# A decoder trunk on one core: the first modulation is loaded at once, summed in fp32, and the transposes of x run two steps ahead

## The chip, the core and the metric

The kernel runs on one core of one Trainium2 chip. The metric is the device time of one execution in microseconds (us); the median of three runs before the change was 2686.47 us, from 2685.94 to 2688.24. The core has a matrix engine (PE, with its weight loads shown apart as PEld), a vector engine (DVE), a scalar engine (ACT), a further engine for general work (POOL, hardly used here) and a queue that issues transfers (SP, shown as SPq). Each engine takes its instructions in the order in which they were written down for it, and waits on semaphores for the others.

## What is computed

Two residual layers. Each has a token mixer (a gated spatial mixer, then dilated attention) and a squared-ReLU MLP, and each of these four sub-layers is modulated by a vector that is computed from c:

```python
def ada_mod(c, w, b):
    m = jax.nn.silu(c) @ w + b
    shift, scale, gate = jnp.split(m, 3, axis=-1)
    return shift[:, None, :], scale[:, None, :], 1.0 + gate[:, None, :]

# first mixer
shift, scale, gate = ada_mod(c, ada_w[i, 0], ada_b[i, 0])
h = x * (1.0 + scale) + shift
uv = jax.nn.gelu(h @ w_in + b_in)
u, v = jnp.split(uv, 2, axis=-1)
v = layer_norm(v, vn_g, vn_b)
...
return (u * z) @ w_out
```

x is 1024 tokens by 1024 features, c has 1024 values, `ada_w[0, 0]` is 1024 by 3072, `w_in` is 1024 by 2048; everything is fp32.

## The kernel before

Everything is tiled by 128: x as eight row tiles `x_0` to `x_7` (128 tokens by 1024), the features as KD = 8 blocks k. Large products are made on PE in three matmuls, with each fp32 operand cut into a high and a low part (`split`, line 104: ACT rounds the high part to the matrix type `fp32r`, DVE subtracts it): high by high, high by low, low by high (`TERMS`). The change is in the first stage of `mixer_a` alone, before and during the products of v (`v_sum`, L475, PSUM tiles `psv`).

What happens there, in order:

- **Modulation columns** (`mods`, L501 on). The first sub-layer's shift and scale are needed as columns (a feature per partition). For each half h of the features, eight tiles of `ada_w` (128 by 2 by 512, 512 KB each: shift and scale side by side) are loaded into a pool of six buffers `adaw`, and DVE adds them up with the weights silu(c): `adaacc += adaw * silu_c[k]` (L509, L511). What is left is a sum over the 128 partitions. `adaacc` is split, and `mod_cols` (L114) lets PE do the sum: eight matmuls for each of shift and scale, with 128 by 128 of `adahi` or `adalo` as the weights and two columns of ones as the moving side (L119, L120, PSUM tiles `psa`), followed by a small addition of the bias on DVE (L124, tiles `ada`).
- **Bias columns.** c and the 64 rows of the biases `ada_b` are loaded into one tile `rows_c`, transposed together on PE (`rows_ct`) and copied to `cols_c`; silu(c) waits for that.
- **Warm-up.** When tile k = 4 of the first half is there, ACT copies a part of it (L513) and PE multiplies it 26 times by ones into a bank that nobody reads (`warm`, L516). These 26 stand in the order written down, ahead of the sums.
- **Transposes and products.** For each block k, PE transposes x (`pst`, L227, four tiles of 128 by 128, or two), ACT applies scale and shift (`h`, L232), ACT rounds (`hT` high, L107), DVE subtracts (`hT` low, L108), and PE multiplies by the weights `winv` of v (L475). `build_hT` does this for one k at a time; the caller alternates it with `v_sum` (`advance`). Two PSUM banks (`tr`) take the transposes and the sums `psa`. Tiles 0 to 3 come first, for k = 0 to 3 (which need the first half of the modulation alone), then tiles 4 and 5 between the loads of the second half, then its sums, then k = 4 to 7 for tiles 0 to 5, then tiles 6 and 7.
- **Row columns.** `rows` (the norms' weights and some biases) is transposed (`rows_t`, L548) and copied to `cols` (L549) near the end of the second half's loads.

The program is written in a framework whose scheduler sets each engine's order from its own estimates; instructions marked `keep_in_program_order` stay in the order in which they were written. After the products of v come the products of u, the spatial mixing, the output projection, the first MLP, attention and the second MLP; the change leaves their code alone.

## Time and profile before

| what | value |
|---|---|
| median of three runs | 2686.47 us |
| the profiled execution's own time | 2688.41 us |
| its span in the profile | 2686.7 us |
| PE busy | 2648.8 us (99%) |
| DVE busy | 1985.0 us (74%) |
| ACT busy | 1383.5 us (51%) |
| first matmul of the products of v | 26.25 us after the span's start |
| first matmul of the products of u | 134.3 us after the span's start |

How to read what follows: a row of a timeline gives the start in us, the length in us, the engine, the line, the operation, the tile written and the tiles read, the shapes, how many follow each other, and in brackets the idle time before it with what ended it. A row of a table of stretches gives the stretch, its length, the busy time of PE, PEld, DVE, ACT and POOL (with the number of instructions), the granted clock of PE (1.00 is full), the share of the transfer engines, and GB/s. PE's matmuls are pipelined, so a row's length is longer than the pace: the pace is read from the starts.

### The profile page before, as it was taken

What the parts mean: (1) busy time and instruction counts of PE and PEld (TensorE: products, weight loads), DVE (VectorE), ACT (ScalarE), POOL (GpSimd) and SP (SyncE); (2) the same over time, 40 slices, a digit from 0 to 9 for tenths busy, and PEclk for the clock granted to TensorE, in tenths of its full rate; (3) what the DMA queues carried; (4) which work ended last, traced back from release to release, by engine and by line L of the source; (5) the groups of instructions that cost most, each with busy time, mean ns of one, the idle gap of its engine ahead of it and who ended that gap; (6) DMA issues with size and microseconds to landing.
All of it is one profiled execution on the core that took longest, in us unless ns stands there. A gap on an engine that the chain in (4) does not pass through costs nothing.

```text
span 2686.7 us, 36966 instructions
## 1 busy us (share of the span) xinstructions
PE 2648.8 (99%) x13204; PEld 2187.0 (81%) x13204; DVE 1985.0 (74%) x3582; ACT 1383.5 (51%) x2626; POOL 103.3 (4%) x189
## 2 busy tenths in 40 slices
PE   7999999999999999999999999999999999999998
PEld 6888878788888888888888888888877788888887
DVE  5896797787888888555556777777658966577877
ACT  3354475555444564433436666666656655553332
POOL 0000000000000001111110000000010000000000
PEclk9999999999999999999999999999999999999999
DMA  7643346777967645655565544554783654495562
GB/s 275 188 149 94 118 146 226 225 234 256 356 209 253 219 165 188 220 188 180 178 216 157 148 137 130 139 147 136 230 220 111 207 201 157 145 313 192 180 208 83
DMA packets 335069, 505.29 MB, mean 188 GB/s; under 512 B 51692, under 2 KB 168852, under 8 KB 334884
## 3 DMA queue, kind: packets, MB, share of 16 engines
q1 hardware_dynamic: 318500, 444.20, 52.1%
q0 software_dynamic: 16384, 58.73, 6.1%
q8 instruction: 103, 1.69, 0.3%
q14 instruction: 82, 0.67, 0.1%
HBM read 365.92 MB, written 136.92 MB: 187 GB/s over the span
## 4 chain that ended last, share of the span: by engine, by line
PE 86%; DVE 8%; DMA 3%; ACT 2%; issue 1%; SPq 0%; DVEq 0%; ACTq 0%
PE psd L1007 22%; PE psv L1336 13%; PE psua L845 9%; PE psk L1437 7%; PE psq L1437 6%; PE psuc L845 4%; PE psu L636 3%; PE psv L475 3%; PE pv L1606 3%; PE psd_wout L391 3%; PE sc L1526 3%; DMA adaw<-in_ada_w_dram 2%; PE psub L845 2%; PE pT L1579 1%; DVE left L108 1%
## 5 line engine op out<-in xcount | busy, mean ns | idle before, releaser
L845 PE MATMUL psua<-right,left 128*128 128x512 f32 x1536 | 365.5, 391 | 2.3 <-DVE right L108 1.7
L1007 PE MATMUL psd<-rhi,lhi 128*128 128x512 f32 x896 | 349.7, 390 | 0.0
L1007 PE MATMUL psd<-rlo,lhi 128*128 128x512 f32 x896 | 348.8, 389 | 0.0
L1007 PE MATMUL psd<-rhi,llo 128*128 128x512 f32 x896 | 348.6, 389 | 0.0
L845 PEld LDWEIGHTS psua<-right,left 128*128 128x128 f32 x1536 | 286.2, 188 | 67.2 <-DVE right L108 4.2
L1548 ACT ACTIVATE p<-p,stat 128x128 f32<-128x128 f32 (+1 forms) x384 | 168.7, 441 | 97.0 <-DVE stat L1546 97.0
L1007 PEld LDWEIGHTS psd<-rhi,lhi 128*128 128x128 f32 x896 | 168.2, 188 | 35.8 <-ACT part L876 0.9
L1007 PEld LDWEIGHTS psd<-rhi,llo 128*128 128x128 f32 x896 | 168.2, 188 | 35.2
L1007 PEld LDWEIGHTS psd<-rlo,lhi 128*128 128x128 f32 x896 | 168.2, 188 | 34.5
L845 PE MATMUL psuc<-right,left 128*128 128x512 f32 x768 | 188.1, 392 | 0.3 <-ACT part L850 0.2
L845 PEld LDWEIGHTS psuc<-right,left 128*128 128x128 f32 x768 | 142.7, 188 | 33.0 <-DVE right L108 1.8
L108 DVE TENSOR_TENSOR pTlo<-pT,pThi 128x512 fp32r<-128x512 f32 (+1 forms) x160 | 99.3, 621 | 76.5 <-ACT pThi L107 75.5
L107 ACT CAST left<-ws 128x512 fp32r<-128x512 f32 x128 | 79.4, 621 | 139.4 <-DVE ws L765 101.8
L108 DVE TENSOR_TENSOR llo<-lraw,lhi 128x1024 fp32r<-128x1024 f32 x112 | 136.4, 1219 | 2.3 <-ACT lhi L107 2.3
L108 DVE TENSOR_TENSOR left<-ws,left 128x512 fp32r<-128x512 f32 x128 | 88.1, 690 | 65.7 <-ACT left L107 63.5
L144 DVE SCALAR_TENSOR_TENSOR adaacc<-adaw,silu_c,adaacc 128x512 f32<-128x512 f32 x140 | 104.6, 747 | 42.2 <-DMA adaw<-in_ada_w_dram 41.4
L1437 PE MATMUL psk<-form_L,wqk_hi 128*128 128x512 f32 x384 | 126.9, 412 | 0.0
L1437 PE MATMUL psq<-form_L,wqk_hi 128*128 128x512 f32 x384 | 126.4, 410 | 0.0
L1336 PE MATMUL psv<-vrhi,form_S 128*128 128x512 f32 x384 | 119.9, 390 | 1.1 <-DVE vpart L1302 0.6
L107 ACT CAST lhi<-lraw 128x1024 fp32r<-128x1024 f32 x112 | 117.2, 1048 | 7.2 <-PE psd L1007 3.3
L1546 DVE CUSTOM_DVE_ANT_0 p<-sc,bias 128x128 f32<-128x128 f32 (+1 forms) x384 | 113.6, 346 | 7.0 <-PE sc L1526 6.8
L107 ACT CAST pThi<-pT 128x512 fp32r<-128x512 f32 (+1 forms) x160 | 84.8, 530 | 62.3 <-PE pT L1579 45.3
(333 smaller groups left out, 6075.8 us busy)
## 6 DMA issues: line engine op xcount, KB each, us to landing
lraw<-forms SPq DMA_DIRECT2D x112, 512.0 KB
adaw<-in_ada_w_dram SPq DMA_DIRECT2D x160, 256.0 KB
up<-in_mlp_w_up_dram SPq DMA_DIRECT2D x64, 512.0 KB
forms<-s SPq DMA_DIRECT2D x128, 256.0 KB
rraw<-in_mlp_w_down_dram SPq DMA_DIRECT2D x64, 512.0 KB
forms<-part SPq DMA_DIRECT2D x96, 256.0 KB
v<-vs POOLq DMA_DIRECT2D x48, 512.0 KB, 3.6
vraw<-in_b_w_qkv_dram SPq DMA_DIRECT2D x42, 512.0 KB
```

Source lines behind the costliest of these rows:

```text
L107: first = A.copy(hi, src) if hi_engine is A else hi_engine.tensor_copy(hi, src)
L108: return first, lo_engine.tensor_tensor(lo, src, hi, op=ALU.subtract)
L144: ins = V.scalar_tensor_tensor(acc[:], raw[:], silu_c[:, k : k + 1], acc[:], ALU.mult, ALU.add)
L391: T.matmul(p[:], stat[a][:, k, o : o + P], u[b][:, w], start=n == 0, stop=n == count - 1)
L475: T.matmul(sums[i][:], hT[half][a_][:, k, o : o + P], units[c, k // 2][b_][:, n : n + HALF], start=k + a_ + b_ == 0, stop=k == KD - 1 and ...
L636: T.matmul(p[:], wu[a_][:, k * P : (k + 1) * P], hT[half][b_][:, k, :], start=k + a_ + b_ == 0, stop=k == KD - 1 and a_ == 1)
L845: T.matmul(acc, w[:, a, k, :], right[p][:, b, k, :], start=p in (1, 2, 5) and k + a + b == 0, stop=k == 3 and a == 1, skip_group_check=True)
L1007: ins = T.matmul(sums[kind, m][:], l[a][:, k, m * P : (m + 1) * P], r[b][:, k, :], start=p in (1, 5, 2, 3) and kp + k + a + b == 0, stop=k ...
L1336: T.matmul(acc, rows[:, m * P : (m + 1) * P], cols_, start=p in (1, 2, 5) and kp + k + a + b == 0, stop=kp == 1 and k == 1 and a == 1, ski ...
L1437: T.matmul(p[:], wu[a][:, k * P : (k + 1) * P], h_op(k, half, b), start=k + c_ == 0, stop=k == KD - 1 and c_ == 2)
L1546: V.tensor_tensor_reduce(out=pr, in0=banks[e][:, sl], in1=st["bias"][:, width - w :], scale=-0.125, scalar=3e38, op0=ALU.add, op1=ALU.min, ...
L1548: A.activation(pr, pr, AF.Exp, bias=nm, scale=-1.0, accum_out=l)
```

## The change

The diff does five things.

- The eight `ada_w` tiles of the first half go into `vz` (the tile that later holds v and is still unused), so that none of the loads waits for a buffer. Those of the second half have the six buffers `adaw` to themselves.
- c and the biases come in two transfers and two transposes: `rows_c` holds c alone, the biases go into `rows_b`, are loaded behind tile 5, transposed as `rows_bt` and copied to a tile `cols_b` of their own.
- The sums over the partitions are plain fp32 matmuls on `adaacc` itself, with one column of ones (`one`): four for each of shift and scale instead of eight, and no split. Both go into one PSUM bank instead of two.
- The warm-up waits for tile 3 instead of tile 4.
- `in_turn` replaces `advance`: the transposes, h and hT of step m + 2 are written behind the products of step m, tiles 4 and 5 following on tiles 0 to 3 in one sequence. The first transpose of each step is kept in program order.

The core of the diff:

```diff
-        nc.sync.dma_start(rows_c[KD : KD + 64, :], ada_b.rearrange("i s (q p) -> (i s) q p", p=P)[:, 0 : 2 * KD, :])
+            if lo is None:
+                T.matmul(pst[:, 2 * k : 2 * k + 1], hi[:, w], one[:], start=True, stop=True)
+                continue
             T.matmul(pst[:, 2 * k : 2 * k + 2], hi[:, w], ones_r[:, 0:2], start=True, stop=False)
             T.matmul(pst[:, 2 * k : 2 * k + 2], lo[:, w], ones_r[:, 0:2], start=False, stop=True)
...
+            def in_turn(*runs):
+                todo = [(i0, n, k) for i0, n, ks in runs for k in ks]
+                gens = {(i0, n): rows_of(i0, n)(ks) for i0, n, ks in runs}
+                def rows(m):
+                    if m < len(todo):
+                        next(gens[todo[m][:2]])
+                rows(0)
+                rows(1)
+                for m, (i0, n, k) in enumerate(todo):
+                    for i in range(i0, i0 + n):
+                        v_sum(0, i, k)
+                    rows(m + 2)
+                    yield
...
-                        raw = ada0.tile([P, 2, HALF], F32, name=f"adaw_0_{h}_{k}", tag="adaw", bufs=6)
+                        raw = ada0.tile([P, 2, HALF], F32, name=f"adaw_0_{h}_{k}", tag="adaw", bufs=6) if h else \
+                            vz[:, k, :].rearrange("p (t n) -> p t n", t=2)
...
-                        if h == 0 and k == 4:
+                        if h == 0 and k == 3:
                             A.copy(warm, raw[:, 0, :])
...
-                    for part in (1, 0):
-                        split(hi[:, part, :], lo[:, part, :], acc[:, part, :])
-                    for part in (1, 0):
-                        mod_cols(0, part, h, bank("tr", f"psa_{part}_{h}"), hi[:, part, :], lo[:, part, :])
+                    p = bank("tr", f"psa_{h}")
+                    for part in (1, 0):
+                        mod_cols(0, part, h, p[:, 8 * part : 8 * part + 8], acc[:, part, :])
...
+                def bias_cols():
+                    nc.sync.dma_start(rows_b[0:64, :], ada_b.rearrange("i s (q p) -> (i s) q p", p=P)[:, 0 : 2 * KD, :])
+                    pt = bank("tr", "rows_bt")
+                    T.transpose(pt[:, 0:P], rows_b[:], ident[:])
+                    V.tensor_copy(cols_b[:], pt[:, 0:64])
-                mods(0)
+                mods(0, {5: [bias_cols]})
```

Beyond the products of v's first half and the first products of its second half, PE, DVE, ACT and SP have the same instructions in the same order as before. Inside that part the order moves. Three places matter.

**DVE, first half of the modulation.** The names: `adaacc` is the running sum, `vz` in the new rows is a tile of `ada_w`. Before:

```order
L80 COPY cols_c<-rows_ct 128x72
L83 TENSOR_TENSOR silu_c<-cols_c,sg 128x8
L509 TENSOR_SCALAR adaacc_144<-adaw_0_0_145,silu_c 128x1024
L511 SCALAR_TENSOR_TENSOR adaacc_144<-adaw_0_1_148,silu_c,adaacc_144 128x1024
L511 SCALAR_TENSOR_TENSOR adaacc_144<-adaw_0_2_151,silu_c,adaacc_144 128x1024
L511 SCALAR_TENSOR_TENSOR adaacc_144<-adaw_0_3_154,silu_c,adaacc_144 128x1024
L511 SCALAR_TENSOR_TENSOR adaacc_144<-adaw_0_4_157,silu_c,adaacc_144 128x1024
L511 SCALAR_TENSOR_TENSOR adaacc_144<-adaw_0_5_188,silu_c,adaacc_144 128x1024
L511 SCALAR_TENSOR_TENSOR adaacc_144<-adaw_0_6_191,silu_c,adaacc_144 128x1024
L511 SCALAR_TENSOR_TENSOR adaacc_144<-adaw_0_7_194,silu_c,adaacc_144 128x1024
L108 TENSOR_TENSOR adalo_198<-adaacc_144,adahi_197 128x512 x2
```

and after, on the same engine:

```order
L81 COPY cols_c<-rows_ct 128x8
L84 TENSOR_TENSOR silu_c<-cols_c,sg 128x8
L533 TENSOR_SCALAR adaacc_150<-vz,silu_c 128x1024
L535 SCALAR_TENSOR_TENSOR adaacc_150<-vz,silu_c,adaacc_150 128x1024 x5
L557 COPY cols_b<-rows_bt 128x64
L535 SCALAR_TENSOR_TENSOR adaacc_150<-vz,silu_c,adaacc_150 128x1024 x2
L128 SCALAR_TENSOR_TENSOR ada_1_0_204<-psa_199,cols_b 128x4
```

A copy out of PSUM (`cols_b<-rows_bt`) now stands between tile 5 and tile 6 of the sum, and the subtraction of the split is gone.

**PE at the same place.** Before (`psa_0_203` and `psa_0_214` are scale and shift; the rows go on with the low parts in turn):

```order
L79 MATMUL rows_ct<-ident,rows_c 128x128
L516 MATMUL warm<-hT_1_0_131,ones_r 128x512 x26
L119 MATMUL psa_0_203<-ones_r,adahi_197 128x2
L119 MATMUL psa_0_214<-ones_r,adahi_197 128x2
L120 MATMUL psa_0_203<-ones_r,adalo_198 128x2
```

and after:

```order
L80 MATMUL rows_ct<-ident,rows_c 128x128
L540 MATMUL warm<-hT_1_0_133,ones_r 128x512 x26
L556 MATMUL rows_bt<-ident,rows_b 128x128
L121 MATMUL psa_199<-one,adaacc_150 128x1 x8
L231 MATMUL pst_0_0_230<-ident,x_0_139 128x128
```

The transpose of the biases stands behind the 26 warm-up matmuls and ahead of the sums; the last four of the eight sums wait for DVE a second time, for the `ada` of the first four, since both share a bank.

**DVE and PE around the second half of the modulation.** Before, on DVE:

```order
L511 SCALAR_TENSOR_TENSOR adaacc_337<-adaw_1_6_425,silu_c,adaacc_337 128x1024
L108 TENSOR_TENSOR hT_1_1_132<-h_4_2_381,hT_1_0_131 128x256
L108 TENSOR_TENSOR hT_1_1_132<-h_4_3_403,hT_1_0_131 128x256
L511 SCALAR_TENSOR_TENSOR adaacc_337<-adaw_1_7_428,silu_c,adaacc_337 128x1024
L549 COPY cols<-rows_t 128x128
L108 TENSOR_TENSOR adalo_432<-adaacc_337,adahi_431 128x512 x2
```

After, on DVE:

```order
L109 TENSOR_TENSOR winv_3_lo<-winv_3_raw,winv_3_hi 128x1024
L109 TENSOR_TENSOR hT_1_1_134<-h_4_3_373,hT_1_0_133 128x256
L575 COPY cols<-rows_t 128x128
L535 SCALAR_TENSOR_TENSOR adaacc_298<-adaw_1_6_404,silu_c,adaacc_298 128x1024
L535 SCALAR_TENSOR_TENSOR adaacc_298<-adaw_1_7_407,silu_c,adaacc_298 128x1024
L128 SCALAR_TENSOR_TENSOR ada_1_1_415<-psa_410,cols_b 128x4
```

and after, on PE:

```order
L574 MATMUL rows_t<-ident,rows 128x128
L479 MATMUL psv_4_346<-winv_1_hi,hT_1_0_133 128x512
L479 MATMUL psv_4_346<-winv_1_lo,hT_1_0_133 128x512
L479 MATMUL psv_5_350<-winv_1_hi,hT_1_0_133 128x512
L479 MATMUL psv_4_346<-winv_1_hi,hT_1_1_134 128x512
L479 MATMUL psv_5_350<-winv_1_lo,hT_1_0_133 128x512
L479 MATMUL psv_5_350<-winv_1_hi,hT_1_1_134 128x512
L121 MATMUL psa_410<-one,adaacc_298 128x1 x4
L231 MATMUL pst_0_4_436<-ident,x_0_139 128x128
L231 MATMUL pst_0_4_436<-ident,x_1_140 128x128
L231 MATMUL pst_0_4_436<-ident,x_2_141 128x128
L121 MATMUL psa_410<-one,adaacc_298 128x1 x4
```

The copy `cols<-rows_t` stood behind the last tile of the sum and now stands ahead of its last two; the transpose that it waits for stands six products ahead of the sums `psa`.

48 lines of the change are left out of this document (22 added, 26 removed).

## The prediction

> **What bounds the kernel now.** I read the page's first part, then the stretches of the first 100 us, then the timelines of the engines there.
>
> ```profile
> PE 2648.8 (99%) x13204; PEld 2187.0 (81%) x13204; DVE 1985.0 (74%) x3582; ACT 1383.5 (51%) x2626; POOL 103.3 (4%) x189
> 0.00:20.00 20.00, 7.15 (x22) 5.58 (x23) 11.49 (x16) 3.25 (x5) 0.70 (x6) 1.00 0.88 310
> 20.00:40.00 20.00, 19.37 (x96) 15.66 (x95) 14.12 (x18) 10.01 (x16) 0.00 (x0) 0.91 1.01 359
> 40.00:60.00 20.00, 19.32 (x85) 15.71 (x84) 9.00 (x15) 9.77 (x16) 0.00 (x0) 0.83 0.74 235
> 60.00:80.00 20.00, 18.34 (x87) 14.04 (x86) 13.56 (x23) 11.26 (x24) 0.00 (x0) 1.00 0.36 112
> 80.00:100.00 20.00, 20.00 (x98) 16.34 (x98) 19.35 (x31) 10.15 (x18) 3.26 (x4) 1.00 0.54 163
> ```
>
> PE is the bound: of 2686.7 us it is idle for 37.9, and 12.85 + 0.63 + 0.68 + 1.66 = 15.8 of these lie in the first 80 us. From 80 us on it is full, and from a little later its order is unchanged, so what the first stage gains or loses on PE should reach the end whole. The granted clock is below 1 in two of the stretches; that is the other loss here. PE's timeline shows the places:
>
> ```profile
> 13.30 8.04 PE L516 MATMUL warm<-hT,ones_r 128*128 128x512 f32 x26 [7.62 <-ACT hT L513]
> 21.18 0.28 PE L119 MATMUL psa<-ones_r,adahi 128*128 128x2 f32 x2
> 26.25 0.78 PE L475 MATMUL psv<-winv_hi,hT 128*128 128x512 f32 x1
> 45.57 0.27 PE L548 MATMUL rows_t<-ident,rows 128*128 128x128 f32 x1
> 46.95 0.25 PE L119 MATMUL psa<-ones_r,adahi 128*128 128x2 f32 x1
> 47.40 0.25 PE L119 MATMUL psa<-ones_r,adahi 128*128 128x2 f32 x1
> 48.26 0.35 PE L120 MATMUL psa<-ones_r,adalo 128*128 128x2 f32 x1
> 48.48 0.35 PE L119 MATMUL psa<-ones_r,adahi 128*128 128x2 f32 x1
> 48.90 4.01 PE L227 MATMUL pst<-ident,x 128*128 128x128 f32 x16
> 52.57 0.78 PE L475 MATMUL psv<-winv_hi,hT 128*128 128x512 f32 x1
> 57.52 0.61 PE L475 MATMUL psv<-winv_hi,hT 128*128 128x512 f32 x2
> 63.64 0.61 PE L475 MATMUL psv<-winv_hi,hT 128*128 128x512 f32 x2
> 72.00 0.60 PE L227 MATMUL pst<-ident,x 128*128 128x128 f32 x4
> ```
>
> The reader should see two stretches without products, 21.18 to 26.25 and 45.57 to 52.57, in which sums, transposes, h and hT follow one another with nothing beside them. Four stretches show the clock's edges:
>
> ```profile
> 23.80:24.00 0.20, 0.20 (x3) 0.20 (x4) 0.20 (x1) 0.20 (x1) 0.00 (x0) 0.95 0.82 317
> 27.20:27.40 0.20, 0.20 (x2) 0.15 (x1) 0.20 (x2) 0.20 (x1) 0.00 (x0) 0.52 0.98 358
> 47.80:48.00 0.20, 0.20 (x3) 0.20 (x3) 0.16 (x1) 0.00 (x0) 0.00 (x0) 0.69 0.00 0
> 54.60:54.80 0.20, 0.20 (x3) 0.16 (x2) 0.00 (x0) 0.20 (x1) 0.00 (x0) 0.75 0.98 338
> ```
>
> The rows are stretches of 0.2 us; 0.95 means that the clock was at half for a tenth of it. So it falls to half at 23.98, 2.8 us after the warm-up, and at 47.86, 2.3 us after the last product, and comes back at 27.39 and 54.70, 1.1 and 2.1 us after products resume. The sums do not hold it up.
>
> **Loads at once.** The transfers were already full:
>
> ```profile
> 1.76 0.80 SPq L74 DMA_DIRECT2D rows_c<-in_ada_b_dram  x1
> 7.21 2.04 SPq L507 DMA_DIRECT2D adaw<-in_ada_w_dram  x2
> 4.00:5.00 1.00, 0.00 (x0) 0.00 (x0) 0.00 (x0) 0.00 (x0) 0.00 (x0) 1.00 0.67 159
> 8.00:9.00 1.00, 0.00 (x0) 0.00 (x0) 0.86 (x1) 0.00 (x0) 0.00 (x0) 1.00 1.02 324
> 12.63 0.62 ACT L513 CAST hT<-adaw 128x512 fp32r<-128x512 f32 x1 [6.43 <-DMA adaw<-in_ada_w_dram]
> 10.07 5.27 DVE L511 SCALAR_TENSOR_TENSOR adaacc<-adaw,silu_c,adaacc 128x1024 f32<-128x1024 f32 x4 [1.22 <-DMA adaw<-in_ada_w_dram]
> 15.93 2.60 DVE L511 SCALAR_TENSOR_TENSOR adaacc<-adaw,silu_c,adaacc 128x1024 f32<-128x1024 f32 x2 [0.59 <-DMA adaw<-in_ada_w_dram]
> ```
>
> SP's wait for a buffer at 7.21 starves nothing: the engines' share is 1.02 right after it. What is gained is the issue of the biases, 0.80 us, which now stands behind tile 5 and left the hole of 0.67 at 4 to 5 us. The warm-up waits for tile 3 instead of 4: tiles 2 and 4 landed at 10.07 and 12.63, so one tile is worth 1.28. Together the warm-up starts 2.1 earlier, at 11.2, and if it takes as long as before, PE is free at 21.18 - 2.1 = 19.1. Cost of the other transfers: nothing, as they keep their order behind the same bytes; the SP queue waits for `winv` buffers as before.
>
> **The first new wait.** PE could do the sums at 19.1, but DVE cannot have finished adding. The copy of the biases stands between tiles 5 and 6, and waits for a transpose that is queued behind all 26 warm-up matmuls. The same kind of pair, `rows_t` and its copy, is the price:
>
> ```profile
> 45.88 0.29 DVE L549 COPY cols<-rows_t 128x128 f32<-128x128 f32 x1 [0.79 <-PE rows_t L548]
> 22.28 0.16 DVE L124 SCALAR_TENSOR_TENSOR ada<-psa,cols_c 128x4 f32<-128x4 f32 x1 [1.76 <-PE psa L120]
> ```
>
> 19.1 + 0.31 (45.57 to 45.88) + 0.29 = 19.7, then tiles 6 and 7, 2.60: DVE ends at 22.3 instead of 18.53, and the first sum starts at 22.4 instead of 21.18. The removed split costs nothing now and saves nothing: it lay under the warm-up.
>
> **The sums in fp32.** Before, 32 matmuls at a pace of 0.113 us at full clock (four from 46.95 to 47.40) and 0.215 at half (48.26 to 48.48). No row shows a plain fp32 matmul that isn't a transpose. One pass, as for these rows, is the lower end; the upper end is both operands in two parts, four products, 0.45 and 0.86. I take three products, 0.34 and 0.645, because the nearest thing the trace has to a product of two uncut fp32 operands is the kernel's own, three matmuls for each (L475). The clock is at half by then: the warm-up ends at 19.1, and 2.8 later is 21.9. So 8 x 0.645 = 5.2. Between shift and scale PE waits for DVE's `ada`, a matmul's length 0.25 + 0.16 + two hand-overs of 0.05, about 0.5. The sums end at 28.1. The first four transposes stand behind them (0.25 each at half clock, by the row of 16, + 0.25 until the result is there): 29.3. Then ACT:
>
> ```profile
> 21.59 1.05 ACT L107 CAST winv_hi<-winv_raw 128x1024 fp32r<-128x1024 f32 x1 [0.18 <-DMA winv_raw<-in_a_w_in_dram]
> 50.11 1.64 ACT L232 ACTIVATE h<-pst,ada,ada 128x512 f32<-128x512 f32 x2 [3.85 <-PE pst L227]
> 51.65 1.12 ACT L107 CAST hT<-h 128x512 fp32r<-128x512 f32 x2
> ```
>
> h 0.82, the second `winv` cast, which ACT's new order has between h and hT, 1.05, and hT 0.56: the first product starts at 31.8 instead of 26.25, **+5.5**. With one pass it is 28.3 (+2.1), with four products 33.5 (+7.3).
>
> On the price, the Trainium skill ("FP8 and Floating Point Precision", TensorE Precision Notes) says that true fp32 takes four passes through the array. By it the upper end holds, and the sum is that of the first rival below; no run shown here bears it out or contradicts it.
>
> **Products, tiles 0 to 5, k = 0 to 3.** Before 45.57 - 26.25 = 19.32. After: 72 matmuls at 0.227 (27 from 57.52 to 63.64), 16.3; 16 transposes at 0.11 (the four at 72.00: 0.60 less one's length of 0.27, by three), since eight of the sixteen that stood ahead of the first product now stand between products, 1.8; half of about 1.6 us at half clock, 0.8; `rows_t` 0.1. That is 19.0, **-0.3**. The stalls before each group vanish, but the transposes that come in take their place:
>
> ```profile
> 38.81 0.89 PE L227 MATMUL pst<-ident,x 128*128 128x128 f32 x4 [0.44 <-ACT h L232]
> 65.65 0.89 PE L227 MATMUL pst<-ident,x 128*128 128x128 f32 x4 [0.50 <-ACT h L232]
> 73.38 0.44 PE L227 MATMUL pst<-ident,x 128*128 128x128 f32 x2 [0.77 <-ACT h L232]
> ```
>
> **The second new wait.** DVE's last two tiles of the second half now stand behind `cols<-rows_t`, and `rows_t` on PE stands six products, 1.36 us, before the products' end E. DVE: E - 1.36 + 0.31 + 0.29 + 2.60 = E + 1.85; before, the last of these tiles had ended just ahead of `rows_t`:
>
> ```profile
> 43.81 1.28 DVE L511 SCALAR_TENSOR_TENSOR adaacc<-adaw,silu_c,adaacc 128x1024 f32<-128x1024 f32 x1
> 46.09 1.28 DVE L108 TENSOR_TENSOR adalo<-adaacc,adahi 128x512 fp32r<-128x512 f32 x2
> ```
>
> So the split's wait (until 47.37) is replaced by one of the same size. Four sums, at full clock until E + 2.5 and at half after it, end at E + 3.95; three transposes fill the hand-over, 0.75; four more sums, 2.6, E + 7.3; `ada` 0.45; h, h, hT 0.82 + 0.82 + 0.56 and 0.1: E + 10.05. Before 52.57 - 45.57 = 7.0: **+3.05** (one pass -0.5, four products +4.75).
>
> **The rest of the stage**, 52.57 to 72.00 = 19.43: 16.3 + 16 transposes 1.8 + half clock 0.8 + 0.5 for DVE, which now has gelu's neighbours ahead of hT: 19.4, **0**. Tiles 6 and 7 begin as before with their first two steps bare (the 0.77 stays). After that PE is full either way.
>
> **Sum**: 5.5 - 0.3 + 3.05 + 0 = +8.3. The profiled execution took 2688.41 (span 2686.7 + 1.7 around), 1.9 above the median; the sum is a difference, so it goes on the median: 2686.5 + 8.3 = **2694.8**.
>
> **Rivals.**
> 1. Four products for an fp32 matmul: 7.3 - 0.3 + 4.75 = +11.75, 2698.2. For it: an uncut operand on both sides; against it: one column of ones needs no second part.
> 2. One pass at half clock: 2.1 - 0.3 - 0.5 = +1.3, 2687.8. Or three products, but with the clock falling late: the first sums 2.7 at full clock, so the first product at 29.3 (+3.1), and in the second place E + 7.85 (+0.85): +3.65, 2690.1. For it: the low clock lasted 3.41 us (23.98 to 27.39) and 6.84 us (47.86 to 54.70), once and twice the same, as if it were judged in steps of 3.4 us; then 2.3 and 2.8 after the last dense work are two draws, and a fall up to 6.8 after it, the end of the first whole step without work, is possible. Against it: both draws were early, and it cannot stay up, since PE is without products for over 7 us. The Trainium skill ("TensorE: Matmul & The Clock Gate", What's actually happening) says that the clock is judged in windows of about 3.4 us that run free of the program; the two widths agree.
> 3. The change doesn't slow the kernel: a sum is one pass, and so short that the clock falls only behind the first sums. First product at 27.0 (+0.75), -0.3, and E + 6.05 in the second place (-0.95): -0.5, 2686.0. It decides when an fp32 sum costs under 0.2 us. For it: `psa`'s rows show that the pace doesn't depend on two columns; against it: those are rows of the matrix type, for which the kernel cuts its operands.
> 4. The first part doing nothing (transfers hidden anyway) is in the sum already.
>
> **Chances.** 0.2% of 2686.5 is 5.4 us, about what a measurement of this kernel can tell from no change: slower means above 2691.9. My forecast 0.42, of which 0.04 stays below 2691.9; rival 1 0.24; rival 2 0.16; rival 3 0.07; gains that I don't see, such as the idles at 72 to 74 us closing and DVE's first wait being shorter, 0.08; losses above 2700 0.03. Faster: 0.08. Same: 0.16 + 0.07 + 0.04 = 0.27. Slower: 0.38 + 0.24 + 0.03 = 0.65. The range reaches from just under rival 3, 2685.5, to 2700, rival 1 with 2 us for a clock that comes back later; it leaves out about 0.13. The likeliest case alone spans 2691 to 2698.
>
> **What would show it.** The copy to `cols_b` waiting several us for PE and the last two tiles of the sum behind it, the first sum after 22 us; the starts of `psa` giving the price; the granted clock at 0.50 through them; first `psv` near 32; `psa` of the second half starting about 2 us after the products end; no idle before the transposes in between. I am wrong if an fp32 sum is a one-pass matmul, if the clock falls late, or if PE's later idle time swallows the delay.

## The result: slower by 0.5%

| | before | after |
|---|---|---|
| median of four runs, us | 2687.02 (2685.94 to 2688.24) | 2699.35 (2698.19 to 2702.61) |
| ratio after/before, 95% interval | | 1.0052, 1.0041 to 1.0064 |
| profiled execution, us | 2688.41 (span 2686.7) | 2698.19 (span 2696.5) |
| half clock in the first 100 us of the profile, us | 10.24 | 17.07 |
| first product of v | 26.25 | 30.17 |
| 72nd product (the last of tiles 0 to 5 before the second sums) | 45.34 | 50.63 |
| first product after the second sums | 52.57 | 58.06 |
| 144th product (the last of tiles 0 to 5) | 71.77 | 78.42 |
| 288th product | 110.73 | 119.31 |
| 384th product (the end of v) | 133.91 | 142.46 |

The medians differ by 12.3 us, the two profiled executions by 9.8. The forecast was +8.3 with a range up to 2700.0: the side was right, the size was too small, and the ratio applied to 2686.47 gives 2700.4, just above the range. "n-th product" is the start of the n-th matmul of `psv` in a profile; between the 72nd and the next, the second sums stand.

The first part of the page of after, and its stretches:

```profile
PE 2653.1 (98%) x13205; PEld 2189.0 (81%) x13205; DVE 1981.7 (73%) x3581; ACT 1382.1 (51%) x2622; POOL 104.0 (4%) x189
...
0.00:20.00 20.00, 8.79 (x26) 6.77 (x27) 8.22 (x14) 2.11 (x3) 0.70 (x6) 1.00 0.90 314
20.00:40.00 20.00, 15.45 (x66) 12.73 (x65) 10.18 (x13) 7.08 (x10) 0.00 (x0) 0.74 0.79 268
40.00:60.00 20.00, 16.72 (x81) 12.93 (x81) 12.70 (x18) 8.46 (x15) 0.00 (x0) 0.87 0.62 209
60.00:80.00 20.00, 19.22 (x89) 15.10 (x87) 9.67 (x17) 10.94 (x20) 0.00 (x0) 0.95 0.51 176
80.00:100.00 20.00, 19.16 (x94) 14.74 (x94) 15.92 (x27) 12.91 (x23) 1.16 (x2) 1.00 0.55 169
100.00:120.00 20.00, 19.06 (x86) 15.44 (x85) 17.18 (x26) 3.76 (x7) 1.79 (x3) 1.00 0.56 168
```

Between 20 and 40 us PE was busy for 15.45 us where it had 19.37, and at 0.74 of the full clock where it had 0.91. Between 80 and 120 us, where PE was full before, it is idle for 0.84 + 0.94 = 1.78 us. PE's busy time also grew, by 4.3 us, with one matmul more: the same work, more of it at half clock.

PE's timeline of after, the rows that answer to those of before:

```profile
11.66 8.95 PE L540 MATMUL warm<-hT,ones_r 128*128 128x512 f32 x26 [6.79 <-ACT hT L537]
20.44 0.27 PE L556 MATMUL rows_bt<-ident,rows_b 128*128 128x128 f32 x1
23.54 1.23 PE L121 MATMUL psa<-one,adaacc 128*128 128x1 f32 x8 [2.83 <-DVE adaacc L535]
25.03 1.86 PE L121 MATMUL psa<-one,adaacc 128*128 128x1 f32 x8 [0.26 <-DVE ada L128]
26.75 1.95 PE L231 MATMUL pst<-ident,x 128*128 128x128 f32 x8
30.17 0.79 PE L479 MATMUL psv<-winv_hi,hT 128*128 128x512 f32 x1 [1.47 <-ACT hT L108]
...
52.87 1.02 PE L121 MATMUL psa<-one,adaacc 128*128 128x1 f32 x8 [1.84 <-DVE adaacc L535]
...
58.06 0.79 PE L479 MATMUL psv<-winv_hi,hT 128*128 128x512 f32 x1 [1.43 <-ACT hT L108]
...
78.65 0.60 PE L231 MATMUL pst<-ident,x 128*128 128x128 f32 x4
80.84 0.50 PE L479 MATMUL psv<-winv_hi,hT 128*128 128x512 f32 x1 [1.59 <-ACT hT L108]
...
105.55 0.50 PE L170 MATMUL psa<-adahi,ones_r 128*128 128x512 f32 x1 [0.94 <-ACT adahi L108]
```

The reader should see the two waits for DVE ahead of `psa` (2.83 and 1.84 us), and that eight sums take 8 + 8 rows: an fp32 sum is two matmuls, at a pace of 0.11 us each at full clock and 0.215 at half.

DVE's timeline of after shows what the two waits are:

```profile
20.75 0.22 DVE L557 COPY cols_b<-rows_bt 128x64 f32<-128x64 f32 x1 [5.01 <-PE rows_bt L556]
20.89 2.60 DVE L535 SCALAR_TENSOR_TENSOR adaacc<-vz,silu_c,adaacc 128x1024 f32<-128x1024 f32 x2
...
49.59 0.42 DVE L109 TENSOR_TENSOR hT<-h,hT 128x256 fp32r<-128x256 f32 x1
49.92 0.28 DVE L575 COPY cols<-rows_t 128x128 f32<-128x128 f32 x1
50.12 2.60 DVE L535 SCALAR_TENSOR_TENSOR adaacc<-adaw,silu_c,adaacc 128x1024 f32<-128x1024 f32 x2
```

The first copy waits 5.01 us for PE. The second waits for nothing; more on that at the second experiment. The clock's edges in after, by stretches of 0.2 us (it falls in the first and third row and comes back in the second and fourth):

```profile
24.20:24.40 0.20, 0.20 (x3) 0.20 (x3) 0.00 (x0) 0.00 (x0) 0.00 (x0) 0.67 0.88 184
34.40:34.60 0.20, 0.20 (x2) 0.14 (x2) 0.00 (x0) 0.00 (x0) 0.00 (x0) 0.73 1.11 379
54.90:55.10 0.20, 0.20 (x3) 0.20 (x3) 0.00 (x0) 0.00 (x0) 0.00 (x0) 0.72 0.00 0
61.70:61.90 0.20, 0.20 (x2) 0.20 (x1) 0.00 (x0) 0.00 (x0) 0.00 (x0) 0.71 1.11 430
```

It is half from 24.27 to 34.51 and from 54.99 to 61.81. After the first product it stays half for 4.3 us (1.1 before), after the first of the second part for 3.7 us (2.1 before).

### The profile page after: what moved, and what is told of

It is laid out like the page before. It is cut to its first block, busy times and chain, and to the rows that moved or that the text cites. A ratio compares the mean times of both kernels' runs of the same rounds, so it can differ in the third digit from the quotient of the medians.

```text
span 2696.5 us, 36953 instructions
## 1 busy us (share of the span) xinstructions
PE 2653.1 (98%) x13205; PEld 2189.0 (81%) x13205; DVE 1981.7 (73%) x3581; ACT 1382.1 (51%) x2622; POOL 104.0 (4%) x189
## 4 chain that ended last, share of the span: by engine, by line
PE 68%; issue 17%; DVE 7%; DMA 4%; ACT 2%; POOL 2%; SPq 0%; POOLq 0%; DVEq 0%; ACTq 0%
PE psd L1028 19%; PE psua L866 10%; PE psk L1458 7%; PE psq L1458 6%; PE psuc L866 5%; PE pv L1627 3%; PE psd_wout L395 3%; PE sc L1547 3%; PE psv L479 3%; PE psub L866 2%; PE psu L657 2%; DMA adaw<-in_ada_w_dram 2%; PE pT L1600 1%; POOL v L1334 1%; PE psoa L1831 1%
## 5 line engine op out<-in xcount | busy, mean ns | idle before, releaser
L109 DVE TENSOR_TENSOR llo<-lraw,lhi 128x1024 fp32r<-128x1024 f32 x112 | 136.1, 1217 | 2.3 <-ACT lhi L108 2.3
```

The source lines that it names most:

```text
L109: return first, lo_engine.tensor_tensor(lo, src, hi, op=ALU.subtract)
```

## The experiments

Four groups of theories are tested. A: what costs are PE's waits, which DVE's order sets. B: the fp32 sums cost. C: the order of products and transposes costs ("the turns" below: `in_turn`). D: what costs is the half clock. All kernels were timed against runs of the kernel before on the same chip (medians there 2682.8 to 2685.4 us). "Half" is the time at half clock in the first 100 us of the kernel's profile, "384th" the start of the last product of v there (132.5 and 132.4 in two further profiles of the kernel before or its like, 133.9 in the first).

| kernel | ratio to before, 95% | us against before | 384th, us | half, us |
|---|---|---|---|---|
| before, profiled first | | | 133.91 | 10.24 |
| before_again | 1.0000, 0.9992 to 1.0009 | 0.0 | 132.55 | 6.83 |
| after | 1.0052, 1.0041 to 1.0064 | 14.0 | 142.46 | 17.07 |
| again (after once more) | 1.0053, 1.0040 to 1.0067 | 14.2 | 143.74 | 20.48 |
| bias_late | 1.0037, 1.0024 to 1.0051 | 9.9 | 138.74 | 13.65 |
| both_late | 1.0033, 1.0020 to 1.0046 | 8.9 | 138.65 | 13.65 |
| fill | 1.0043, 1.0030 to 1.0056 | 11.5 | 137.87 | 10.24 |
| split | 1.0051, 1.0039 to 1.0064 | 13.7 | 141.66 | 17.07 |
| t67 | 1.0037, 1.0024 to 1.0050 | 9.9 | 139.58 | 17.07 |
| late_t67 | 1.0027, 1.0016 to 1.0037 | 7.2 | 135.23 | 13.65 |
| late_t67_fill | 1.0026, 1.0015 to 1.0036 | 7.0 | 135.33 | 10.24 |
| loads | 1.0017, 1.0009 to 1.0026 | 4.6 | 137.61 | 13.65 |
| sums | 1.0017, 1.0008 to 1.0026 | 4.6 | 133.59 | 6.83 |
| turns | 1.0020, 1.0011 to 1.0029 | 5.4 | 137.32 | 13.65 |
| loads_sums_late | 1.0009, 0.9999 to 1.0018 | 2.4 | 133.24 | 6.83 |
| lsl_64 | 1.0007, 0.9997 to 1.0017 | 1.9 | 132.78 | 3.41 |
| lsl_64_fill | 1.0001, 0.9992 to 1.0010 | 0.3 | 131.24 | 0.00 |
| delay | 1.0000, 0.9991 to 1.0009 | 0.0 | 132.91 | 0.00 |
| before_32 | 1.0005, 0.9996 to 1.0014 | 1.3 | 132.43 | 6.83 |
| after_64 | 1.0046, 1.0033 to 1.0058 | 12.3 | 142.65 | 17.07 |

The third column is the ratio less one, times the median of the kernel before on that chip; an interval of 0.0009 to each side is 2.4 us. "Half" counts from the first record of the clock, which lies between 13.76 and 18.26 us, when the clock comes up during the warm-up. The warm-up does not start at the same time in every execution (10.50 to 13.45 us over the 20 profiles), so a part of a difference between two profiles can lie there.

### The wait for the biases (bias_late)

DVE's copy of the biases is written behind the eighth tile and kept there; DVE, PE and ACT are otherwise as in after.

```diff
                     rows_bt.append(bank("tr", "rows_bt"))
                     T.transpose(rows_bt[0][:, 0:P], rows_b[:], ident[:])
-                    V.tensor_copy(cols_b[:], pt[:, 0:64])
-                mods(0, {5: [bias_cols]})
+                mods(0, {5: [bias_cols], 7: [lambda: tc.keep_in_program_order(V.tensor_copy(cols_b[:], rows_bt[0][:, 0:64]))]})
```

> The changed kernel, with DVE's copy of the biases moved behind the eighth tile of the first sum; nothing else moves. Theory A (the waits cost): the eighth tile is added by 19 us, the first sum starts right behind the transpose of the biases at 20.8 instead of 23.5, the first product comes 3 to 4.5 us earlier (near 26), and the whole is 3.5 to 5 us less than the changed kernel: 8 to 9.5 us above the kernel before. Theory D (what costs is the half clock, whose windows run free): the first product comes earlier as in A, but the clock falls all the same, more of the products are done at half clock, and of the 3.5 to 5 us half or less arrives: 10 to 13 us above the kernel before.

DVE's timeline and PE's, of this kernel:

```profile
9.25 9.21 DVE L535 SCALAR_TENSOR_TENSOR adaacc<-vz,silu_c,adaacc 128x1024 f32<-128x1024 f32 x7
20.86 0.23 DVE L562 COPY cols_b<-rows_bt 128x64 f32<-128x64 f32 x1 [2.40 <-PE rows_bt L560]
```

```profile
20.55 0.27 PE L560 MATMUL rows_bt<-ident,rows_b 128*128 128x128 f32 x1
20.66 0.95 PE L121 MATMUL psa<-one,adaacc 128*128 128x1 f32 x8
21.86 1.05 PE L121 MATMUL psa<-one,adaacc 128*128 128x1 f32 x8 [0.26 <-DVE ada L128]
```

The eighth tile is added at 18.46, the first sum starts at 20.66, the first product at 25.73 instead of 30.17, and both groups of sums run at full clock. Of these 4.4 us 3.7 are left at the 384th product (138.74 against 142.46), and 4.1 in the ratio (14.0 less 9.9). The gain is the 3.5 to 5 us of A, though the 9.9 lies between A's 8 to 9.5 and D's 10 to 13, and the interval of the ratio covers both. The wait was real, and it is the larger of the two waits; one stretch of 3.41 us at half clock went with it (13.65 us instead of 17.07).

### The wait for `cols` (both_late)

The copy `cols<-rows_t` too is put behind the eighth tile, of the second sum.

```diff
-                then[4].append(row_cols)
+                then[7] = [row_cols]
```

> As the last, and the copy of the transposed rows of ln and biases also behind the eighth tile of the second sum. Theory A: the 1.8 to 2.7 us in which PE waits for DVE at 51 us vanish too, the second sums start within 0.3 us of the end of the first products, 6 us above the kernel before (5 to 7.5). Theory D: 9 to 11 us above it, as the shorter gap does not save a window of half clock.

It gained nothing: 0.09 us at the 384th product. PE still waited 1.64 us, as DVE's and PE's timelines of this kernel show:

```profile
45.79 0.42 DVE L109 TENSOR_TENSOR hT<-h,hT 128x256 fp32r<-128x256 f32 x1
46.12 2.60 DVE L535 SCALAR_TENSOR_TENSOR adaacc<-adaw,silu_c,adaacc 128x1024 f32<-128x1024 f32 x2
48.64 0.28 DVE L578 COPY cols<-rows_t 128x128 f32<-128x128 f32 x1
```

```profile
48.87 1.02 PE L121 MATMUL psa<-one,adaacc 128*128 128x1 f32 x8 [1.64 <-DVE adaacc L535]
```

So the copy was not the cause of more than 0.2 us of it, and theory A was wrong here on the mechanism; the 8.9 in the total is near D's 9 to 11. In DVE's order the last two tiles stand behind `winv_lo` and the subtraction for the last `hT` of tiles 4 and 5; with or without the copy they start about 1 us before the products end, and take 2.60. DVE's queue is at fault, but with other instructions in it. Where the tiles stand ahead, in the kernel sums (below), they are done before the products end:

```profile
44.87 2.59 DVE L516 SCALAR_TENSOR_TENSOR adaacc<-adaw,silu_c,adaacc 128x1024 f32<-128x1024 f32 x2
47.38 0.42 DVE L110 TENSOR_TENSOR hT<-h,hT 128x256 fp32r<-128x256 f32 x1
```

There the gap from the last product to the next is 53.24 - 48.68 = 4.6 us; here it is 53.67 - 47.23 = 6.4, in after 58.06 - 51.02 = 7.0. That the place of the tiles makes this difference is read from the comparison; no run moves the tiles alone.

### Work in PE's waits (fill)

The waits of after stay; 12, 6 and 10 matmuls that nobody reads are put into them.

```diff
+                    for _ in range(12 if h == 0 else 10):
+                        tc.keep_in_program_order(T.matmul(pw[:] if h == 0 else p[:, P:HALF], ones_r[:], warm if h == 0 else warm[:, P:HALF], start=True, stop=True))
...
                 rows(0)
                 rows(1)
+                if fill:
+                    for _ in range(6):
+                        tc.keep_in_program_order(T.matmul(fill[0][:], ones_r[:], warm, start=True, stop=True))
```

> The changed kernel with its waits as they are, but matmuls of the warm-up's kind put into them: 12 behind the transpose of the biases, 6 behind the first eight transposes of x, 10 narrower ones ahead of the second sums; their results are not used. Theory D: the clock stays up or is half in one window of 3.4 us instead of five, the first sums and transposes take half the time (first product 1 to 2 us earlier), the products' first 4 us and the 3.7 us after 58 run at full clock: 5 to 6 us less than the changed kernel, 6.5 to 8 us above the kernel before. Theory A: PE's waits are as long, so nothing is gained: 12 to 14 us above the kernel before.

Half clock fell from 17.07 to 10.24 us, the first product came at 27.39, and the 384th 4.6 us earlier than in after. But 2.24 us of that were there before any of the added matmuls could matter. This execution had begun its warm-up 1.05 us earlier, at 10.61, and its clock came up as early as 13.76, so that DVE had the biases and the sum sooner and the first sum started at 21.30 instead of 23.54:

```profile
18.22 3.06 PE L548 MATMUL warm<-hT,ones_r 128*128 128x512 f32 x12
21.30 1.05 PE L121 MATMUL psa<-one,adaacc 128*128 128x1 f32 x8
27.39 0.41 PE L479 MATMUL psv<-winv_hi,hT 128*128 128x512 f32 x1
```

```profile
18.65 2.60 DVE L538 SCALAR_TENSOR_TENSOR adaacc<-vz,silu_c,adaacc 128x1024 f32<-128x1024 f32 x2
```

From the first sum to the 384th product fill gains 2.35 us on after, without any wait taken away, and as much is seen in the total (14.0 less 11.5 = 2.5, with intervals that overlap). That is about half of D's 5 to 6; the 11.5 lies between D's 6.5 to 8 and A's 12 to 14. The fillers ahead of the second sums did not keep the clock up (half from 51.31 to 58.13). Late in the run a wait for a transfer was 4.5 us long here (2.24 in after), with 6.83 us of half clock behind it. D holds for a part of the first stage; in the whole it is not resolved.

### The order for tiles 6 and 7 (t67)

Only this loop gets the old order back, not pinned.

```diff
-            for _ in in_turn((6, 2, range(KD))):
+            gen = rows_of(6, 2, pinned=False)(range(KD))
+            for k in range(KD):
+                next(gen)
+                for i in (6, 7):
+                    v_sum(0, i, k)
                 tick()
```

> The changed kernel with the old order for tiles 6 and 7 alone, where the scheduler may again put products of v's second half between them. Theory A: from the 144th to the 288th product it takes 39.0 us, as in the kernels before, loads and sums, where all kernels with turns took 40.9; the total falls by 2 us: 10 to 11 us above the kernel before. If the order there is not the cause: 40.9 again and 12 to 13 us above it.

From the 144th to the 288th product it took 116.43 - 77.50 = 38.93 us. In the kernel before this is 110.73 - 71.77 = 38.96, in after 119.31 - 78.42 = 40.89. That is the 39.0 expected, and the total falls to 9.9 (10 to 11 expected). PE is full again; stretches of t67:

```profile
80.00:100.00 20.00, 20.00 (x99) 16.05 (x100) 18.29 (x31) 12.81 (x23) 1.72 (x3) 1.00 0.60 185
100.00:120.00 20.00, 20.00 (x90) 16.52 (x89) 16.49 (x26) 3.69 (x6) 1.47 (x2) 1.00 0.54 171
```

Where the scheduler is free it puts products of v's second half between those of tiles 6 and 7, and PE has something to do while ACT makes `hT` and `adahi`. With the steps pinned in turn it waits 1.78 us in these 40 us. All 20 profiles show the 2 us: each kernel that has the turns for tiles 6 and 7 took 40.8 to 41.0 us there, each without them 38.8 to 39.0.

### Each part alone (loads, sums, turns)

Three kernels put one part of the change on the kernel before: loads (the first modulation in `vz`, the biases apart, the warm-up at tile 3), sums (fp32, no split), turns (`in_turn` in all its places).

```diff
+                            vz[:, k, :].rearrange("p (t n) -> p t n", t=2)
...
-                        if h == 0 and k == 4:
+                        if h == 0 and k == 3:
...
-                mods(0)
+                mods(0, {5: [bias_cols]})
```

```diff
-                    for part in (1, 0):
-                        split(hi[:, part, :], lo[:, part, :], acc[:, part, :])
+                    p = bank("tr", f"psa_{h}")
+                        mod_cols(0, part, h, p[:, 8 * part : 8 * part + 8], acc[:, part, :])
```

```diff
-                gen = rows_of(0, 4)(first_ks)
-                for k in first_ks:
-                    advance(gen, k, range(4))
+                turns = in_turn((0, 4, first_ks), (4, 2, first_ks))
...
+            for _ in in_turn((6, 2, range(KD))):
```

> Only the loads part on the kernel before: first modulation into the region of v, biases loaded and copied apart between tiles 5 and 6, warm-up after tile 3; split sums and the old order stay. Theory A (the loss comes from the copy of the biases, which makes DVE wait for a transpose behind the warm-up, and from the low clock that follows): the last two tiles end near 23.5 us as in the changed kernel, the split then stands bare behind them, the first sum starts at 24.2 or later instead of 21.2, all sums are at half clock, the first product comes 4 to 6 us later than before: 2691.5 us (2690 to 2694). Theory B (the loss comes from the uncut fp32 sums): this kernel has none, it starts earlier: 2684 to 2687. Theory C (the loss comes from the products in turn): the same as B.

> Only the fp32 sums on the kernel before, without splits. Theory A: the first sum still starts at 21.2 behind the warm-up, eight sums take 1.8 at full clock or 3.5 at half where sixteen matmuls and two results took 3.9; the second place loses the split of 1.3 us and starts its sums right behind the products: 2 to 3 us less in all, 2684 us (2682.5 to 2687, the clock's windows making up the width). Theory B: 2692 us or more. Theory C: 2686.5.

> Only the transposes two steps ahead of the products on the kernel before, in the order that pins them. Theory A: the first products start with eight transposes instead of sixteen ahead of them, 0.5 to 1 us earlier, and the stage of tiles 0 to 5 is otherwise as long; the stage of tiles 6 and 7 with the start of v's second half is 1.5 to 3 us longer, because the products of the other half no longer fill PE's waits for ACT: 2688 us (2686.5 to 2690). Theory B: 2686.5. Theory C: 2692 us or more, with the loss in the first 80 us.

Loads alone: 4.6 us, as A said, with the first product at 31.09 and 13.65 us of half clock. Against B: this kernel has no fp32 sum. Sums alone: the first product at 25.58 and the second gap 4.6 us instead of 6.8, as A said, and the 384th product 0.3 us before that of the first profile, 1.0 behind that of the second; the total was nevertheless 4.6 us up, which neither A nor B had (B's 5 us would have stood in the first stage). Turns alone: 5.4, where A had about 1.5 and C 5.5 or more. The 2 us at tiles 6 and 7 are there (114.13 - 73.21 = 40.92); for the other part half clock is seen. Before, sixteen transposes stood ahead of the first product, and the clock came back 1.1 us after it; with eight, PE has pauses there, and the clock comes back at 30.29, 5.0 us after the first product (25.24). But the number of transposes does not decide it alone: sums and loads_sums_late (below) have the old order, and the clock came back 4.9 us after their first product.

Behind the second gap the difference is plain. In all eleven profiles of kernels with the turns the first products there run at half clock, for 3.2 to 6.05 us; in the nine with the old order they don't, but for the first profile of before, with 2.1.

The three parts add up to 4.6 + 4.6 + 5.4 = 14.6 us, where the whole change has 14.0 and 14.2; each of them is known to about 2.4.

### The sums undone (split)

After with the split and the two-column matmuls of the kernel before.

```diff
-                        mod_cols(0, part, h, p[:, 8 * part : 8 * part + 8], acc[:, part, :])
+                    hi, lo = (ada0.tile([P, 2, HALF], F32R, name=f"ada{m}_{h}", tag="adaw", bufs=6) for m in ("hi", "lo"))
+                        split(hi[:, part, :], lo[:, part, :], acc[:, part, :])
+                        mod_cols(0, part, h, bank("tr", f"psa_{part}_{h}"), hi[:, part, :], lo[:, part, :])
```

> The changed kernel with the fp32 sums undone: the split into two parts and sixteen two-column matmuls for eight sums, as before; loads and turns stay. Theory A: the split now stands bare behind the last tiles in both places and the sums are twice as many matmuls: 2 to 5 us more than the changed kernel, 15 to 18 us above the kernel before. Theory B (the fp32 sums are a cost): 2 to 5 us less than the changed kernel, 8 to 11 us above the kernel before.

Neither: 13.7 us, as after. The first product came 0.8 us later (30.98), the second gap was 4.8 us instead of 7.0, since the scheduler now put the last two tiles earlier on DVE. So within after the sums are neither a cost nor a gain that can be seen; a few us either way stay possible, since the intervals reach 3 us and more to each side. Why sums alone were 4.6 us up is not answered by it.

### The change once more (again), and without the turns (loads_sums_late)

> The changed kernel once more, unaltered, to see what repeats. If the half-clock stretch at 1983 us is a chance of where the clock's windows fall against a wait for a transfer: it is absent from this profile or stands elsewhere, the stretches of the first 100 us stay within 1 us of those of the first profile, and the times spread over 2695 to 2701. If the program sets it: half clock from 1983 to 1987 again and 2699 us within 1.

The ratio repeats (1.0053). Over its five runs the mean granted clock was 0.9946, over the 27 of the kernel before on that chip 0.9975; times the span that is 14.6 and 6.8 us, so that up to 7.8 of the 14 us are half clock (less, as far as PE stood idle in it). Repeated, too, is the half clock at 1983 us (from 1982.38, for 6.83 us). It was expected to be absent if it is chance; two of two proves little either way. Over all 20 profiles a stretch of half clock behind v and ahead of the run's end is found in nine, all of kernels with the fp32 sums (of which there are 13), and in none of the seven without. No run says why. The half clock of the first 100 us was one window more than in the first profile, so those stretches don't repeat within 1 us.

loads_sums_late is after with the old order everywhere and the copy of the biases behind the eighth tile (the two diffs above together).

> The changed kernel without the turns (transposes of x in the order of the kernel before) and with the copy of the biases behind the eighth tile: loads at once and fp32 sums, but neither the wait nor the new order. Theory A with D (waits, half-clock windows and the order of the transposes are the whole loss): the first sum at 20.8, the first product near 25.3, the second gap 4.6 to 5 us instead of 7, the last product of the sixth tile's second half near 70 where the kernel before has 71.8, and the products of v's second half 1 to 2 us earlier than there: 1 to 3 us below the kernel before. Theory B (the fp32 sums cost something later in the run that the first 100 us do not show, as the kernel with the sums alone was 4.6 us slower and its first 134 us were not): 2 to 5 us above it.

The first product is at 25.33, the second gap 52.95 - 48.40 = 4.6, the 144th product at 71.16, the 384th at 133.24: without the wait and without the turns the loss in the first stage is gone. A with D expected a gain of 1 to 3 us in all, and none came: the total is 2.4 us up. That is within the 2 to 5 of B in its later form (the sums cost something behind the first stage), though the interval of the ratio reaches down to no change.

### A delay that costs nothing (delay, before_again)

delay is the kernel before with 34 warm-up matmuls instead of 26.

```diff
-                            for _ in range(26):
+                            for _ in range(34):
```

> The kernel before with 34 matmuls in its warm-up instead of 26, so that everything behind it starts 1.8 us later and nothing else changes. If a delay is passed on and no more: 1.8 us above the kernel before (1 to 2.6, a window of half clock more or less making up the width), and what follows the 384th product takes as long as there. If a shift by itself costs more later, by where the later waits fall among the clock's windows: 3.5 to 6 us above it, with the excess behind the 384th product.

> The kernel before, unaltered, for a profile on the same chip and to see what a ratio of two runs of one kernel is: 1.0000, within 0.0007 on each side; in its profile the 384th product at 133.9 us within 1.5, and from there to the end 2547 to 2550 us.

Everything behind the warm-up did start 2.5 us later than in before_again (first sum 23.64 against 21.16; 0.8 of it is a later start of this execution's warm-up), and the total did not change: 1.0000. The profile shows why; stretches of before_again and of delay:

```profile
20.00:40.00 20.00, 19.16 (x95) 15.68 (x94) 13.33 (x16) 9.34 (x16) 0.00 (x0) 0.91 1.00 359
40.00:60.00 20.00, 19.33 (x91) 15.65 (x92) 9.26 (x16) 10.04 (x17) 0.00 (x0) 0.91 0.70 227
```

```profile
20.00:40.00 20.00, 19.42 (x101) 15.73 (x99) 13.79 (x17) 8.47 (x12) 0.00 (x0) 1.00 1.00 344
40.00:60.00 20.00, 18.63 (x94) 14.67 (x95) 9.45 (x16) 11.09 (x20) 0.00 (x0) 1.00 0.72 245
```

In the profile of delay the clock did not fall until the run's end. By the 384th product 2.1 of the 2.5 us were back. The other executions agree: the mean granted clock over the eleven runs of delay was 0.9983, over the 26 of the kernel before on that chip 0.9976, and times the span that is 1.8 us less of half clock. Both expectations had left that out. before_again came out as expected, but its profiled execution was among its slowest (2690.27 us against a median of 2685.74) and took 2556.0 us from the 384th product to the end, where 2547 to 2550 were expected: the part behind v varies by several us with the same kernel (2552.8 in the first profile).

### The shift by 32 bytes (before_32, after_64, lsl_64, lsl_64_fill)

The kernels with the new column of ones lost more than their first stage shows. By the program's allocation (the profiles hold no addresses) that column takes 32 bytes of the constants, and nearly all tiles behind it move by as much. before_32 adds an unused column to the kernel before; after_64 gives the column 64 bytes in after, lsl_64 in loads_sums_late; lsl_64_fill adds four unread matmuls behind the first four transposes.

```diff
-    one = cst.tile([P, 1], F32, name="one")
+    one = cst.tile([P, 16], F32, name="one")
```

> The kernel before with one more column tile of 4 bytes among its constants, set once and never used. It takes a slot of 32 bytes, so that nearly all tiles allocated behind it, which start at multiples of 64 bytes in the kernel before, start 32 bytes behind such multiples, as they do in the changed kernel. Theory S (the shift makes transfers slower, and with them the waits behind the first 140 us longer): the packets' time of the hardware queue rises from about 51.2 to 51.7% of the span, and the whole is 2 to 4 us above the kernel before. If the later waits are chance: within 1 us of it.

> The changed kernel with its column of ones in a tile of 64 bytes instead of 4, of which one column is used, so that the tiles behind it start at multiples of 64 bytes again. Theory S: 2 to 4 us less than the changed kernel, 9 to 11 us above the kernel before, and from the 384th product to the end 2 to 4 us less than in the changed kernel. If the later waits are chance: 12.5 to 14 us above it, as measured twice.

> Loads at once and fp32 sums, transposes in the old order, copy of the biases behind the eighth tile, and the column of ones in 64 bytes. Theory S: the 2.4 us by which the same kernel with the shift was above the kernel before vanish: between 2 us below it and 0.5 above. If the later waits are chance: 2 to 3 us above it again.

> As the last, with four more matmuls of the warm-up's kind behind the first four transposes of x, in the 0.9 us in which PE waits for the first hT. Theory D: the window behind the first sums counts as busy, the clock comes back one window of 3.4 us earlier, and 1 to 1.7 us are gained on the last kernel; without that, it is the same within 0.5 us.

The theory finds no support: 1.3 us with an interval from -1.1 to 3.8 for the shift alone, and 1.7 and 0.5 us between the kernels with and without it, all within the uncertainty; the packets' time of the hardware queue was 51.5 or 51.6% in all four, shifted or not. An effect of one us or a few isn't excluded.

The last pair bears on D. Stretches of lsl_64 and of lsl_64_fill:

```profile
20.00:40.00 20.00, 18.55 (x91) 14.42 (x90) 11.68 (x16) 9.99 (x16) 0.00 (x0) 0.91 0.96 336
```

```profile
20.00:40.00 20.00, 18.75 (x99) 15.02 (x98) 13.32 (x18) 11.44 (x18) 0.00 (x0) 1.00 0.98 336
```

With four matmuls in a pause of 0.9 us the clock stayed up, and the 384th product came 1.5 us earlier. Of that 0.7 is an earlier first sum in this execution (20.50 against 21.19), which leaves 0.85, just below the 1 to 1.7 expected. The totals, 1.9 and 0.3 us, agree but don't settle it. The clock supports it: over eleven runs each the mean granted clock was 0.9987 with the four matmuls and 0.9977 without, which times the span is 2.7 us less of half clock. lsl_64_fill is the fastest kernel with the loads and the sums, and it is as fast as the kernel before, not faster.

### Taken together (late_t67, late_t67_fill)

late_t67 has the copy of bias_late and the loop of t67; late_t67_fill adds six unread matmuls behind the first eight transposes and eight ahead of the second sums.

> The changed kernel with two of its losses taken back: the copy of the biases behind the eighth tile, and the old order for tiles 6 and 7. Loads, fp32 sums and the turns of tiles 0 to 5 stay. If the two add up: the 384th product at 142.5 - 3.7 - 1.95 = 136.8 us (136 to 138), 4 to 6 us above the kernel before in that place and in all 4 to 7 above it. If one hides the other: 138 to 139 us there, 7 to 10 above it.

> As the last, with six matmuls of the warm-up's kind behind the first eight transposes of x and eight narrower ones ahead of the second sums, in places where PE waits. Theory D, that what is left is half clock: the clock stays up, or falls for one window, in the first 60 us; the 384th product at 132.5 to 134.5 us, and in all 0 to 2.5 us above the kernel before. If the order of the turns itself costs as well: 135 us or later there, 3 us or more above it.

The two repairs add up: 135.23 at the 384th product, or 136.1 if the 0.9 us are added by which the first sum started earlier in this execution than in bias_late (19.76 against 20.66); 136.8 was expected. The total, 7.2, is just above its 4 to 7. The filled kernel did not reach its 132.5 to 134.5, and with 135.33 and a total of 7.0 its numbers are those expected if the order of the turns itself costs. Its first half-clock stretch shrank to one window (3.41 us), but the clock fell again at 51.02, and the products behind the second gap ran at half until 57.85. That is 6.05 us at half behind the first of them (51.80), or 3.0 lost, and it is as much as is left against before_again: 2.8 us at the 384th product, 2.8 at the 144th (73.23 against 70.45). So in this profile the turns of tiles 0 to 5 cost through the half clock that goes with them, and no other cost is seen in the first stage. The other 4.2 of the 7.0 us are not seen in the first stage and are not explained.

## Why the prediction was right on the side and short on the size

By its own terms, from the two first profiles:

| term | predicted | measured |
|---|---|---|
| PE free behind the warm-up | 19.1 | 20.44 |
| first sum | 22.4 | 23.54 |
| sums and hand-over | 5.7 | 3.2 |
| first product | +5.5 | +3.9 |
| products of tiles 0 to 5, k 0 to 3 | -0.3 | +1.4 |
| second gap | +3.05 | +0.2 |
| rest of the stage, to 72.00 before and 78.65 after | 0 | +1.15 |
| tiles 6, 7 and the start of v's second half | 0 | +1.9 |
| the rest to the end of the span | 0 | +1.2 |
| sum | +8.3 | +9.8 |

Up to the end of v, two terms that slow the kernel were put too low: the half clock behind the start of the products (0.8 us in each place, 2.15 and 1.85 measured) and the order for tiles 6 and 7 (nothing, 1.9 measured). That the sum came as near as it did is luck, since the price of the sums over the partitions was put too high. What comes on top behind v is told below, and stays open in part.

**The loads.** "If it takes as long as before, PE is free at 19.1" failed: the warm-up took 8.8 us, not 7.9. It starts at half clock, and the clock does not come up a fixed time after its start but at 17.15 before and 17.44 after, so that an earlier start bought mainly slow matmuls. It varies between executions of one kernel (5.78 us after the warm-up's first matmul in after, 4.23 in again), and over the 20 profiles from 3.15 to 6.22 us. Warm-up rows alone, of before and of after:

```profile
12.00:17.00 5.00, 3.70 (x9) 2.94 (x10) 1.00 1.05 401
17.50:20.50 3.00, 3.00 (x15) 2.42 (x14) 1.00 1.05 408
```

```profile
12.00:17.00 5.00, 5.00 (x13) 3.84 (x13) 1.00 1.05 379
17.50:20.50 3.00, 3.00 (x14) 2.17 (x12) 1.00 1.05 387
```

Up to 17.0 a matmul takes about 0.4 us in both, behind it about 0.2 (the clock's column reads 1.00 there, because the records of the clock begin only at 17.15 and 17.44; the pace shows it). Being 1.64 us earlier was worth 0.74.

**The first new wait** was right in place and mechanism, and bias_late shows its price: 4.4 us at the first product.

**The sums** were priced too high. The step that failed is "I take three products": the trace shows two matmuls for a sum. Nor was "the clock is at half by then" right for all of them: the clock fell at 24.27, 3.8 us after the warm-up's end at 20.44 and not 2.8, and the first four sums ran nearly all at full clock. The Trainium skill ("FP8 and Floating Point Precision", TensorE Precision Notes) has four passes for true fp32; the trace shows two matmul rows for a sum, at the pace of the fp32r rows of the kernel before, 0.11 and 0.215 us, and by four the second gap would have been 1.8 us longer at full clock. The first rival, which rested on the price of four, is excluded by these paces, and the measured total came close to its 2698.2 for other reasons.

**The products of tiles 0 to 5** failed at "half of about 1.6 us at half clock". It was 4.3 us and, behind the second gap, 3.7, so 2.15 and 1.85 us of loss instead of 0.8 each. The half clock lasted two and three times 3.41 us here. That the transposes which were moved out of the gap had brought the clock back early before is likely behind the second gap, where all kernels with the turns show it; at the first product it stays open, as sums and loads_sums_late kept those transposes and had two times 3.41 us as well.

**The second new wait** has the right size (PE waits until 1.85 us after the products' end, 1.85 predicted) and the wrong cause: both_late moved the copy away and kept 1.64 us of the wait. The cheap sums hid it: the gap is 7.0 us (51.02 to 58.06) where 6.8 stood before.

**"After that PE is full either way"** failed at tiles 6 and 7, 1.9 us, shown by t67. The prediction had looked at the first two steps of these tiles only, and not at what the scheduler had put between the later ones.

**Behind v** the order is the same, but not the time. In after the wait for `bk<-qk` at 1983 us is followed by 3.41 us at half clock, in which PE was busy throughout, so that it cost half of that, 1.7 us:

```profile
1982.86 1.14 PE L1547 MATMUL sc<-bk,bq 64*128 64x256 f32 x12 [2.24 <-DMA bk<-qk]
...
1983.40:1983.60 0.20, 0.20 (x8) 0.20 (x4) 0.00 (x0) 0.00 (x0) 0.00 (x0) 0.80 1.26 358
```

So the 8.3 was nearly met by the end of v (+8.55), by luck, through errors that cancel: 2.5, 0.3 and 2.85 us too much for the sums, the way from them to the first product and the second gap, against 1.15, 1.7, 1.15 and 1.9 too little for the first sum, the two stretches of products and the order. What was missing in the whole lies in part in the choice of the profile: the profiled execution of before had 10.24 us of half clock, two later ones 6.83 and the 384th product 1.4 us earlier; and that of after was the fastest of four.

**What stays open.** In the first 140 us after loses 8.6 to 11.2 us. Its totals are 12.3 to 14.2 us up. Sums and the kernels built on after have 1.6 to 6 us more than their first 140 us show (after_64 2.2), and not all of that is the clock at 1980 us. For the kernel sums the granted clock of all its runs says the same: 0.9971 against 0.9975 is 1.1 us of half clock, and of the rest of its 4.6 us at most 1.0 is seen up to the 384th product, against before_again. That shifted addresses explain it is not seen. It can be the variation of the later waits: behind v PE stood idle for 12.4, 14.2 and 10.5 us in three profiles of the kernel before or its like (before, before_again, before_32), and for 12.1 and 13.0 in after and again. With one profile and five to eleven runs of a kernel this was not settled.

## What to carry to other kernels

Before moving a copy out of PSUM into the middle of an engine's queue, look at what the transpose that feeds it is queued behind; here one copy of 0.22 us held up 2.6 us of work and cost about 4 us. A pause of PE can cost its length and the half clock behind it, here in steps of 3.41 us: price it so, and look whether the work you move out of a pause (transposes, warm-up) may be what kept the clock up. An order that is pinned takes away the fillers that a scheduler had found; look at what stood in PE's waits before pinning.
